# An MLP in Strassen-Winograd form: a tile of its own for the upper weight block, another row of weight steps, two sums on VectorE, and other places for loads where the up phase turns into the down phase

## The chip, the cores and the metric

The kernel runs on one core of a Trainium2 chip. The metric is the device time of one execution in microseconds; of several runs the median counts, and less is better. The names of the engines in the rows are PE (TensorE), PEld (its weight loads), DVE (VectorE), ACT (ScalarE), POOL (GpSimd) and SP (SyncE, which issues nearly all DMAs).

## What is computed

A trunk of two layers on one sequence of 1024 tokens with 1024 channels, all in float32. A layer has a mixing part and then the MLP, which alone is changed here:

```python
h = rms_norm(x, norm2[l])
x = x + jnp.square(jax.nn.relu(h @ w_up[l])) @ w_down[l]
```

`w_up` is 1024 x 4096 and `w_down` 4096 x 1024.

## The kernel before

**Precision.** Every factor of a product is held as two rounded parts, a high part `h` and a low part `l`, and each product is three matmuls: high x high, low x high, high x low (`mm3`). The helper `split` (lines 155 and 156) makes the parts: ScalarE casts the high part, VectorE subtracts it from the source. So every operand costs one ScalarE and one VectorE instruction.

**Strassen-Winograd.** The MLP multiplies 2 x 2 blocks with seven products in place of eight. `STEPS` lists them: for each step the PSUM bank (X, Y or Z), the weight block and the block of the input. The weight blocks A11, A12 and A22 come as they are; S1 to S4 are sums of raw weight blocks. One raw 128 x 1024 tile holds the upper half (`top`: A11, A12), another the lower half (`low`). `weight_steps` returns the named pieces of this work:

- `load`: two DMAs, 512 KB each, into `raw` tiles (two buffers for both halves together);
- `A1`: split of the upper tile (tile names `wh`, `wl`); `s1_s2`: two sums on GpSimd into `s` (lines 828 and 829); `S12`: split of `s` (`wh`, `wl` again);
- `s3_s4`: two differences on GpSimd (lines 835 and 836), the first into `tmp`, the second over the lower tile itself; `S3`: split of `tmp` (`uh`, `ul`); `S4`: split of the lower tile (`vh`, `vl`).

**The up phase** (`for fp in range(NFP)`, 16 periods a layer, 7 steps of 12 matmuls each, so 84 matmuls). While TensorE works on period `fp`, the other engines make the weights of `fp + 1`; `UP_AT` says behind which step of the period each piece is written. A number above 6 means the next period: 7 is its step 0, 8 its step 1. After each product comes its evacuation: ScalarE copies the first use of a bank out (`keep`, line 990: P1 after step 0, U2 after step 2, P5 after step 3), since a later step accumulates on top in the same bank; VectorE adds or subtracts the next one (lines 1040, 1049, 1053) and applies ReLU times the RMS factor (`relu`, line 996), GpSimd squares the result (line 999). `mixed` (line 1011) makes the blocks T1 to T4 from the four squared blocks B11, B12, B21, B22 with four VectorE sums, and the blocks go to DRAM (`hid`); B11 and B21 are stored as two parts (`in_two`). In the last two periods of layer 1 there are no `mixed` blocks.

Within the up phase the order on ScalarE, VectorE and GpSimd is that of the program: `queue` chains each instruction to the one before on its engine. What waits at the head holds all behind it. Elsewhere, and on SyncE and TensorE, a scheduler sets the order when the program is built.

**The down phase** (`for g`, 8 groups in layer 0 and 7 in layer 1, each of two halves `u` of 14 products of 6 matmuls, so 84 matmuls again). VectorE adds each product to the tiles `acc` (line 1105), which hold the residual stream. `load_block` fetches the blocks of the next group (raw in `hr`, then split into the per-block tiles), and `weight_steps` prepares the weights for the next half by `DOWN_AT`.

**The change of phase.** In the last up period the blocks of the first down group are loaded and split, one pair of blocks after each step. Six `acc` tiles are loaded one period before that (`early_acc`), the other ten when the pool `md` of the down phase opens (line 1112).

**The start of the up phase.** The RMS factors need sums of squares over all channels. `rms(1, 0)` (lines 198 to 216) is written behind step 3 of the first period: TensorE sums columns against `ones` (line 198, waiting for GpSimd's last addition), and after a power on GpSimd it spreads the result (line 214). ReLUs written earlier are put off until then (`after_rms`).

## Time and profile before

| | us |
|---|---|
| median of 3 runs | 2311.51 (2309.04 to 2314.63) |
| the profiled execution | 2312.99 |
| span of the profile | 2311.1 |
| TensorE busy | 2160.8 (93%) |
| VectorE busy | 1777.5 (77%) |
| GpSimd busy | 1181.7 (51%) |
| ScalarE busy | 944.8 (41%) |

The page also cuts the span into 40 slices; TensorE's clock is granted in full in most of them. The mean busy share says little about a kernel of many stages. The up phase lies from 466.57 to 827.74 us in layer 0 and from 1600.98 to 1957.67 in layer 1; the down phase follows each. The views used below are busy time by stretch, timelines of single engines, and lists of who waited for whom.

### The profile page before, as it was taken

The page shows a single profiled execution, that of the slowest core. Times are in us where ns is not written, and L with a number is a line of the kernel's source. Part 1 is how long each engine was busy: PE and PEld are TensorE (multiplying, and loading weights), DVE is VectorE, ACT ScalarE, POOL GpSimd, SP SyncE. Part 2 cuts the span into 40 slices and gives each one's busy share as a digit, 9 for nine tenths or more (in the row PEclk, how much of TensorE's full clock was granted, in tenths as well). Part 3 has the DMA queues.
Part 4 walks back from the last instruction along what each step waited for, and adds up shares of the span by engine and source line. Part 5 has one row for each costly group of instructions (what it writes and reads, how often), then busy time and mean ns, then how long its engine had stood idle before and what let it go on. Part 6 is the DMA issues. An engine that isn't in the chain of part 4 may idle for free. (4 is left out here: it accounts for less than half of the span.)

```text
span 2311.1 us, 30279 instructions
## 1 busy us (share of the span) xinstructions
PE 2160.8 (93%) x10608; PEld 1783.2 (77%) x10608; DVE 1777.5 (77%) x2244; ACT 944.8 (41%) x1669; POOL 1181.7 (51%) x915
## 2 busy tenths in 40 slices
PE   7999999979999979999999999998999999899997
PEld 6988887767777767788788888876777777688886
DVE  8788779976666679888868878799666665988864
ACT  5566562532332233333356656435323223433321
POOL 6455556675555633333455646459555555332315
PEclk9999999989999999999999999999999999999998
DMA  3000112234444486554311010133444446765512
GB/s 129 28 28 28 43 33 87 96 128 165 159 171 152 151 298 223 158 193 145 106 50 39 18 46 25 55 87 119 155 154 156 173 157 221 251 194 179 173 55 73
DMA packets 153737, 283.17 MB, mean 123 GB/s; under 512 B 15089, under 2 KB 48369, under 8 KB 153585
## 3 DMA queue, kind: packets, MB, share of 16 engines
q1 hardware_dynamic: 151920, 279.15, 36.1%
q10 hardware_dynamic: 1664, 2.10, 0.3%
q8 instruction: 83, 1.36, 0.2%
q14 instruction: 70, 0.57, 0.1%
HBM read 190.49 MB, written 90.70 MB: 122 GB/s over the span
## 5 line engine op out<-in xcount | busy, mean ns | idle before, releaser
L434 POOL TENSOR_TENSOR a<-a,s 128x255 f32<-128x255 f32 (+1 forms) x192 | 237.2, 1243 | 183.6 <-ACT a L427 100.9
L828 POOL TENSOR_TENSOR s<-raw 128x512 f32<-128x512 f32 x62 | 95.3, 1537 | 457.4 <-DMA raw<-in_w_down 273.9
L999 POOL TENSOR_TENSOR ct<-ct 128x512 f32<-128x512 f32 x128 | 173.7, 1357 | 208.9 <-DVE ct L996 110.2
L156 DVE TENSOR_TENSOR wl<-raw,wh 128x1024 fp32r<-128x1024 f32 x114 | 168.3, 1477 | 48.3 <-ACT wh L155 48.1
L243 PE MATMUL pj<-hB,wh 128*128 128x512 f32 x504 | 198.4, 394 | 0.9 <-ACT hB L880 0.9
L248 PE MATMUL pj<-lB,wh 128*128 128x512 f32 x504 | 197.6, 392 | 1.0 <-DVE lB L881 1.0
L249 PE MATMUL pj<-hB,wl 128*128 128x512 f32 x504 | 197.2, 391 | 0.0
L1011 DVE TENSOR_TENSOR ct<-ct,ct 128x512 f32<-128x512 f32 x120 | 80.4, 690 | 133.2 <-POOL ct L999 132.1
L1105 DVE TENSOR_TENSOR acc<-acc,po 128x512 f32<-128x512 f32 x240 | 159.1, 679 | 19.2 <-PE po L249 18.0
L155 ACT CAST wh<-raw 128x1024 fp32r<-128x1024 f32 x114 | 119.6, 1049 | 100.1 <-PE pj L248 77.9
L155 ACT CAST wh<-s 128x1024 fp32r<-128x1024 f32 x62 | 65.0, 1049 | 206.8 <-POOL s L829 197.6
L155 ACT CAST ct<-ct 128x512 fp32r<-128x512 f32 x64 | 39.7, 620 | 250.4 <-POOL ct L999 250.4
L458 DVE TENSOR_TENSOR tl<-t,th 128x512 fp32r<-128x512 f32 (+1 forms) x160 | 99.0, 629 | 44.4 <-ACT th L456 43.1
L243 PE MATMUL pg<-hB,vh 128*128 128x512 f32 x240 | 98.2, 409 | 37.0 <-ACT ct L990 36.9
L155 ACT CAST hT<-hr 128x512 fp32r<-128x512 f32 x122 | 74.2, 619 | 139.9 <-DMA hr<-hd_T 90.1
L431 DVE TENSOR_TENSOR_SCAN s<-s 128x256 f32<-128x256 f32 (+3 forms) x128 | 123.4, 976 | 6.4 <-ACT s L426 6.1
L156 DVE TENSOR_TENSOR wl<-s,wh 128x1024 fp32r<-128x1024 f32 x62 | 90.6, 1461 | 40.6 <-ACT wh L155 40.6
L835 POOL TENSOR_TENSOR tmp<-raw,raw 128x512 f32<-128x512 f32 x62 | 121.4, 1959 | 0.0
L243 PE MATMUL po<-hT,wh 128*128 128x512 f32 x256 | 105.4, 412 | 9.2 <-ACT ct L990 4.0
L426 ACT ACTIVATE s<-z 128x256 f32<-128x256 f32 (+1 forms) x192 | 95.4, 500 | 45.4 <-PE z L422 13.6
L248 PEld LDWEIGHTS pj<-lB,wh 128*128 128x128 f32 x504 | 94.9, 188 | 21.1 <-DVE lB L881 1.6
L243 PEld LDWEIGHTS pj<-hB,wh 128*128 128x128 f32 x504 | 94.9, 188 | 20.8 <-ACT hB L880 1.3
(274 smaller groups left out, 7094.7 us busy)
## 6 DMA issues: line engine op xcount, KB each, us to landing
raw<-in_w_up SPq DMA_DIRECT2D x64, 512.0 KB, 3.6
raw<-in_w_down SPq DMA_DIRECT2D x64, 512.0 KB, 3.7
hd_T<-ct SPq DMA_DIRECT2D x120, 256.0 KB, 2.8
hr<-hd_T SPq DMA_DIRECT2D x120, 256.0 KB, 3.1
raw<-in_w_in SPq DMA_DIRECT2D x36, 512.0 KB, 3.7
hd_B<-ct SPq DMA_DIRECT2D x34, 256.0 KB, 2.0
hr<-hd_B SPq DMA_DIRECT2D x34, 256.0 KB, 3.5
raw<-in_w_out SPq DMA_DIRECT2D x16, 512.0 KB, 3.6
```

Of the source, the lines that this page charges most:

```text
L155: queue("act", nc.scalar.copy(hi, src))
L156: queue("dve", nc.vector.tensor_sub(lo, src, hi.bitcast(F32)))
L243: mm = nc.tensor.matmul(ps, ah, bh, start=first and i == 0, stop=False, skip_group_check=more)
L248: nc.tensor.matmul(ps, ah, bl, start=False, stop=False, skip_group_check=more)
L249: mm = nc.tensor.matmul(ps, al, bh, start=False, stop=last and i == n - 1, skip_group_check=more)
L426: nc.scalar.activation(s[:, lo:CH], z[:, 0:w], AF.Sigmoid, scale=-ISQ)
L431: nc.vector.tensor_tensor_scan(sl, sl, sl, 1.0 if prev is None else prev[:, CH - 1 : CH], ALU.mult, ALU.bypass)
L434: nc.gpsimd.tensor_mul(a[:, lo + 1 : CH], a[:, lo + 1 : CH], s[:, lo : CH - 1])
L458: nc.vector.tensor_sub(tl[:, 0:wd], pt[:, 0:wd], th[:, 0:wd].bitcast(F32))
L835: queue("pool", nc.gpsimd.tensor_sub(s3, r["a1"][:, 0], r["a2"][:, 0]))
L999: queue("pool", nc.gpsimd.tensor_mul(t, t, t))
L1105: (nc.vector.tensor_add if sign > 0 else nc.vector.tensor_sub)(x, x, ps)
```

## The change

- The upper weight tile gets its own place `rt` (one buffer, pool `mw`); `raw` keeps two buffers for the lower tile alone. To make room, `hr` has 3 buffers in place of 4, and one `acc` tile fewer is loaded early.
- `weight_steps` takes an engine. In the up phase the two differences `s3_s4` go to VectorE; for the first period's weights and in the down phase they stay on GpSimd.
- `UP_AT` has each piece one or two steps earlier.
- The early `acc` loads move from period 14 to period 12; the ten others are eleven now, three at the opening of `md` and the rest written behind steps 1 to 4 of the first half group.
- The raw blocks T2 (both) and T1 (one) of the first down group are loaded from period 14, step 3; B22 and T4 are loaded and split in the first half group in place of the last up period; the blocks of group 1 are all loaded in the second half of group 0 in place of half by half.
- `rms(1, 0)` is written behind step 5 of the first period in place of step 3, and the ReLU of B22 is put off with the others.

```diff
--- before.py
+++ after.py
@@ -797,10 +797,11 @@
                 b = "T1" if b == "B12" else b
                 return t512("h" + b, 4, F32R, pool), t512("l" + b, 4, F32R, pool)
-            def weight_steps(srcs, n, out):
+            def weight_steps(srcs, n, out, eng="pool"):
+                sub = {"pool": nc.gpsimd, "dve": nc.vector}[eng].tensor_sub
                 turns = "p (n k w) -> p k n w"
                 r = {}
@@ -815,11 +816,11 @@
                     return two
                 def load():
-                    raws = []
-                    for src in srcs:
-                        raws.append(per.tile([P, D], F32, tag="raw", name=nm("raw"), bufs=2))
-                        nc.sync.dma_start(raws[-1].rearrange("p (f c) -> p f c", f=src.shape[1]), src)
-                    r["top"], r["low"] = raws
+                    r["top"] = mw.tile([P, D], F32, tag="rt", name=nm("rt"), bufs=1)
+                    r["low"] = per.tile([P, D], F32, tag="raw", name=nm("raw"), bufs=2)
+                    raws = r["top"], r["low"]
+                    for raw, src in zip(raws, srcs):
+                        nc.sync.dma_start(raw.rearrange("p (f c) -> p f c", f=src.shape[1]), src)
                     r["a1"], r["a2"] = (x.rearrange(turns, n=n, k=2) for x in raws)
                 def s1_s2():
@@ -832,8 +833,8 @@
                 def s3_s4():
                     s3 = r["s3"] = tmp()
                     s3 = s3.rearrange("p (n w) -> p n w", n=n)
-                    queue("pool", nc.gpsimd.tensor_sub(s3, r["a1"][:, 0], r["a2"][:, 0]))
-                    queue("pool", nc.gpsimd.tensor_sub(r["a2"][:, 0], r["s2"], r["a1"][:, 1]))
+                    queue(eng, sub(s3, r["a1"][:, 0], r["a2"][:, 0]))
+                    queue(eng, sub(r["a2"][:, 0], r["s2"], r["a1"][:, 1]))
                 return {
                     "load": load,
@@ -847,7 +848,7 @@
-            UP_AT = {"load": 2, "A1": 3, "s1_s2": 3, "s3_s4": 4, "S12": 5, "S3": 7, "S4": 8}
+            UP_AT = {"load": 0, "A1": 2, "s1_s2": 2, "s3_s4": 3, "S12": 4, "S3": 5, "S4": 7}
             DOWN_AT = {"load": 0, "A1": 2, "s1_s2": 2, "S12": 3, "s3_s4": 4, "S3": 4, "S4": 6}
             def up_blocks(fp):
@@ -931,7 +932,7 @@
             acc_, b_next, early_acc = {}, [], []
             for u in range(2):
-                early_acc += [(2 * u + q, c) for c in ((1, 0), (0,))[u] for q in range(2)]
+                early_acc += [(q, 1 - u) for q in range(2)] + [(2, 0)] * u
             def load_acc(m, c, pool):
                 acc_[m, c] = pool.tile([P, CH], F32, name=nm("acc"))
@@ -941,7 +942,7 @@
                 if b in STORED:
                     return None
-                raw = t512("hr", 4, F32, mw)
+                raw = t512("hr", 3, F32, mw)
                 nc.sync.dma_start(raw, hid[fp, b])
                 return raw
@@ -971,7 +972,7 @@
                 for fp in range(NFP):
                     a, a_next = a_next, {}
-                    work = weight_steps(*(up_blocks(fp + 1) if fp < NFP - 1 else down_blocks(0, 0)), a_next)
+                    work = weight_steps(*(up_blocks(fp + 1) if fp < NFP - 1 else down_blocks(0, 0)), a_next, "dve")
                     todo = {k - 7: v for k, v in left.items() if k > 6}
                     for name, f in work.items():
                         todo.setdefault(UP_AT[name], []).append(f)
@@ -979,7 +980,7 @@
                     banks = {"X": pso(), "Y": psj(), "Z": psg() if fp else pso()}
                     kept, hb = {}, {}
                     classic = l == DEPTH - 1 and fp >= NFP - 2
-                    if fp == NFP - 2:
+                    if fp == NFP - 4:
                         for mc in early_acc:
                             load_acc(*mc, mw)
                     if fp == NFP - 1:
@@ -1025,9 +1026,13 @@
                         bank, i = products(a, xb, banks, step, 0)
                         ps = banks[bank]
                         b = STEPS[step][3]
-                        if fp == NFP - 1:
-                            raws = [raw_block(p, b) for p in range(2)]
-                        if step == 3 and fp == 0:
+                        if (fp, step) == (NFP - 2, 3):
+                            raws = {"T2": [raw_block(p, "T2") for p in range(2)], "T1": [raw_block(0, "T1")]}
+                        if (fp, step) == (NFP - 1, 3):
+                            raws["T1"].append(raw_block(1, "T1"))
+                        if (fp, step) == (NFP - 1, 4):
+                            raws["T3"] = [raw_block(p, "T3") for p in range(2)]
+                        if step == 5 and fp == 0:
                             rms(1, 0)
                             rms_done = True
                             for f, args in later:
@@ -1047,7 +1052,7 @@
                             elif (bank, i) == ("X", 2):
                                 t = kept["P5"]
                                 queue("dve", nc.vector.tensor_sub(t, ps, t))
-                                relu("B22", t, t, 0)
+                                after_rms(relu, "B22", t, t, 0)
                             elif (bank, i) == ("Z", 1):
                                 t = kept["U2"]
                                 queue("dve", nc.vector.tensor_sub(t, t, ps))
@@ -1064,9 +1069,9 @@
                                 mixed("T3", "B22", "B12", nc.vector.tensor_sub)
                             elif step == 6:
                                 mixed("T4", "B21", "T2", nc.vector.tensor_sub)
-                        if fp == NFP - 1:
+                        if fp == NFP - 1 and step < 5:
                             for p in range(2):
-                                b_next[p][b] = load_block(p, b, raws[p])
+                                b_next[p][b] = load_block(p, b, raws[b][p] if b in raws else None)
                 for k in sorted(left):
                     if k > 6:
                         for f in left[k]:
@@ -1105,11 +1110,13 @@
                     (nc.vector.tensor_add if sign > 0 else nc.vector.tensor_sub)(x, x, ps)
                 n_groups = groups - (l == DEPTH - 1)
-                for u in range(2):
-                    for i, c in ((0, 1), (0, 0), (2, 0), (2, 1)):
-                        for q in range(2):
-                            if (4 * u + i + q, c) not in acc_:
-                                load_acc(4 * u + i + q, c, md)
+                for mc in ((3, 0), (2, 1), (3, 1)):
+                    load_acc(*mc, md)
+                first_acc = {
+                    k: [(4 + i + q, c) for q in range(2)] for k, i, c in ((1, 0, 1), (2, 0, 0), (3, 2, 0), (4, 2, 1))
+                }
                 for g in range(n_groups):
                     bs, b_next = b_next, [{}, {}]
                     for u in range(2):
@@ -1142,9 +1149,16 @@
                             for name, f in work.items():
                                 if DOWN_AT[name] == step:
                                     f()
-                            if g < n_groups - 1:
-                                b = STEPS[step][3]
-                                b_next[u][b] = load_block(2 * g + 2 + u, b)
+                            b = STEPS[step][3]
+                            if g == u == 0:
+                                for mc in first_acc.get(step, []):
+                                    load_acc(*mc, md)
+                                if step < 2:
+                                    for p in range(2):
+                                        bs[p][STEPS[step + 5][3]] = load_block(p, STEPS[step + 5][3])
+                            elif g < n_groups - 1:
+                                for p in range(2) if g == 0 else (u,):
+                                    b_next[p][b] = load_block(2 * g + 2 + p, b)
                         if g == groups - 1:
                             if u == 1:
                                 order.pop(0)
```

What this makes of the instruction order is shown at three places.

VectorE, one period in the middle of layer 0's up phase, from the sum that makes B11 (`ct_6392`, now `ct_6396`) on; `rbc` is the RMS factor. Before:

```order
L1040 TENSOR_TENSOR ct_6392<-pj_6378,ct_6392 128x512
L996 SCALAR_TENSOR_TENSOR ct_6392<-ct_6392,rbc_5350 128x512
L156 TENSOR_TENSOR vl_6420<-raw_6289,vh_6419 128x1024
L156 TENSOR_TENSOR ct_6438<-ct_6392,ct_6437 128x512
L156 TENSOR_TENSOR wl_6462<-raw_6443,wh_6461 128x1024
L1049 TENSOR_TENSOR ct_6459<-po_6377,ct_6459 128x512
L996 SCALAR_TENSOR_TENSOR ct_6459<-ct_6459,rbc_5357 128x512
L1053 TENSOR_TENSOR ct_6435<-ct_6435,pg_6379 128x512
L996 SCALAR_TENSOR_TENSOR ct_6435<-ct_6435,rbc_5357 128x512
```

Now:

```order
L1045 TENSOR_TENSOR ct_6396<-pj_6382,ct_6396 128x512
L997 SCALAR_TENSOR_TENSOR ct_6396<-ct_6396,rbc_5391 128x512
L156 TENSOR_TENSOR ct_6442<-ct_6396,ct_6441 128x512
L156 TENSOR_TENSOR wl_6448<-rt_6408,wh_6447 128x1024
L836 TENSOR_TENSOR tmp_6468<-rt_6408,raw_6409 128x512
L837 TENSOR_TENSOR raw_6409<-s_1331_6451,rt_6408 128x4x128
L1054 TENSOR_TENSOR ct_6466<-po_6381,ct_6466 128x512
L997 SCALAR_TENSOR_TENSOR ct_6466<-ct_6466,rbc_5398 128x512
L156 TENSOR_TENSOR wl_6488<-s_1331_6451,wh_6487 128x1024
```

The split of the lower tile (`vl`) has left this piece for an earlier one, and the two differences (lines 836 and 837, out of `rt` and `raw`) stand between `wl` and the sum for B22 (line 1054). The second reads `s`, the product of GpSimd's two sums.

TensorE, start of layer 0's up phase; `pj` and `po` are the banks of steps 1, 0 and 2, `rbc_4785` and `rbc_4807` the sums of squares of the two token halves. Before:

```order
L248 MATMUL pj_5270<-lB_1096_5191,wh_5244 128x512
L249 MATMUL pj_5270<-hB_1095_5190,wl_5245 128x512
L198 MATMUL pg_5329<-ones,rbc_4785 128x2 x4
L198 MATMUL pg_5337<-ones,rbc_4807 128x2 x4
L243 MATMUL po_5269<-hT_1003_4863,wh_5251 128x512
```

Now:

```order
L243 MATMUL po_5269<-hB_984_4787,wh_5244 128x512
L248 MATMUL po_5269<-lB_985_4788,wh_5244 128x512
L198 MATMUL pg_5370<-ones,rbc_4785 128x2 x4
L249 MATMUL po_5269<-hB_984_4787,wl_5245 128x512
L243 MATMUL po_5269<-hB_1018_4906,wh_5244 128x512
```

The column sums of the first half, which stood behind the 24 matmuls of steps 0 and 1, stand behind the second matmul of step 0. Those of the other half stay between steps 1 and 2.

SyncE, the change of phase in layer 0; `acc<-xm` are loads of the residual stream, `hr<-hd` raw blocks (138 to 149 belong to group 1). Before:

```order
L1007 DMA hd_B21l<-ct_7874 128x512
L821 DMA raw_7929<-in_w_down 128x4x256
L945 DMA hr_8168<-hd_T_147 128x512
L938 DMA acc_7887<-xm_1_104 128x512
L938 DMA acc_7889<-xm_1_106 128x512
L938 DMA acc_7891<-xm_1_108 128x512
L938 DMA acc_7893<-xm_1_110 128x512
```

Now:

```order
L823 DMA raw_8058<-in_w_down 128x4x256
L1008 DMA hd_B21l<-ct_7852 128x512
L946 DMA hr_8203<-hd_B_139 128x512
L946 DMA hr_8209<-hd_B_149 128x512
L939 DMA acc_7861<-xm_0_107 128x512
L939 DMA acc_7863<-xm_1_104 128x512
L939 DMA acc_7865<-xm_1_106 128x512
L939 DMA acc_7917<-xm_1_108 128x512
L939 DMA acc_7919<-xm_1_110 128x512
```

All eleven later `acc` loads stand in one row here too (four of them are shown), behind loads of group 1's blocks; the first is `acc_7861`, which the first half group adds to.

## Rows read from the trace of the kernel before

**Rows 1.** Busy us by stretch: from:to length, PE PEld DVE ACT POOL, clock, DMA, GB/s.

```profile
466.57:504.84 38.27, 30.28 (x117) 23.66 (x118) 26.96 (x25) 15.65 (x24) 29.45 (x21) 0.78 0.32 112
504.84:803.75 298.91, 278.80 (x1178) 217.58 (x1176) 192.05 (x238) 87.32 (x126) 167.56 (x112) 1.00 0.47 164
803.75:901.06 97.31, 84.88 (x338) 65.39 (x336) 78.30 (x108) 36.04 (x54) 37.08 (x25) 0.95 0.78 265
1057.15:1076.49 19.34, 19.34 (x85) 15.77 (x84) 16.34 (x21) 6.68 (x9) 7.20 (x4) 1.00 0.60 204
1638.70:1936.95 298.25, 278.66 (x1177) 217.54 (x1176) 191.42 (x238) 87.22 (x126) 168.06 (x112) 1.00 0.47 164
1936.95:2028.67 91.72, 81.91 (x337) 63.19 (x336) 75.78 (x98) 35.88 (x54) 35.05 (x25) 0.98 0.77 261
```

**Rows 2.** Timeline of TensorE, one period of the up phase: start us, us, [idle <-releaser].

```profile
1844.13 0.40 PE L249 MATMUL po<-hT,ul 128*128 128x512 f32 x1
...
1845.85 0.50 PE L243 MATMUL pg<-hB,vh 128*128 128x512 f32 x1 [1.32 <-ACT ct L990]
...
1867.20 0.50 PE L243 MATMUL pg<-hB,vh 128*128 128x512 f32 x1 [1.32 <-ACT ct L990]
```

**Rows 3.** Timeline of GpSimd in that period.

```profile
1847.60 1.59 POOL L828 TENSOR_TENSOR s<-raw 128x512 f32<-128x512 f32 x1 [2.93 <-DMA raw<-in_w_up]
...
1852.30 2.27 POOL L835 TENSOR_TENSOR tmp<-raw,raw 128x512 f32<-128x512 f32 x1
1854.65 1.29 POOL L836 TENSOR_TENSOR raw<-s,raw 128x512 f32<-128x512 f32 x1
1855.90 1.04 POOL L999 TENSOR_TENSOR ct<-ct 128x512 f32<-128x512 f32 x1
...
1864.12 1.90 POOL L999 TENSOR_TENSOR ct<-ct 128x512 f32<-128x512 f32 x1 [3.40 <-issue]
```

**Rows 4.** Timeline of VectorE in that period.

```profile
1846.78 1.23 DVE L156 TENSOR_TENSOR wl<-raw,wh 128x1024 fp32r<-128x1024 f32 x1 [0.74 <-ACT wh L155]
...
1852.01 1.41 DVE L156 TENSOR_TENSOR wl<-s,wh 128x1024 fp32r<-128x1024 f32 x1 [0.57 <-ACT wh L155]
...
1856.98 2.02 DVE L1011 TENSOR_TENSOR ct<-ct,ct 128x512 f32<-128x512 f32 x3 [3.56 <-POOL ct L999]
...
1863.29 0.69 DVE L996 SCALAR_TENSOR_TENSOR ct<-ct,rbc 128x512 f32<-128x512 f32 x1
1863.90 1.22 DVE L156 TENSOR_TENSOR vl<-raw,vh 128x1024 fp32r<-128x1024 f32 x1
```

**Rows 5.** Timeline of ScalarE at the end of that period.

```profile
1866.05 0.62 ACT L155 CAST ct<-ct 128x512 fp32r<-128x512 f32 x1 [3.24 <-POOL ct L999]
1866.57 0.58 ACT L990 COPY ct<-pg 128x512 f32<-128x512 f32 x1
1867.05 1.05 ACT L155 CAST wh<-raw 128x1024 fp32r<-128x1024 f32 x1
```

**Rows 6.** Timeline of the DMA issues from SyncE in that period.

```profile
1843.79 0.33 SPq L821 DMA_DIRECT2D raw<-in_w_up  x1
...
1861.88 0.38 SPq L1007 DMA_DIRECT2D hd_B21h<-ct  x1
...
1865.14 0.33 SPq L821 DMA_DIRECT2D raw<-in_w_up  x1
```

**Rows 7.** The loads of line 821 by source line, whole run.

```profile
DMA to landing us min/median/max: 3.3/3.6/7.6
```

**Rows 8.** Timeline of TensorE in the first up period of layer 0.

```profile
478.49 1.86 PE L198 MATMUL pg<-ones,rbc 128*128 128x2 f32 x8 [2.61 <-POOL rbc L187]
...
485.71 0.80 PE L243 MATMUL po<-hT,wh 128*128 128x512 f32 x1 [2.01 <-ACT ct L990]
```

**Rows 9.** Timeline of TensorE in the first down half group of layer 0.

```profile
838.96 0.78 PE L249 MATMUL po<-hT,wl 128*128 128x512 f32 x1 [3.36 <-DVE wl L156]
```

**Rows 10.** Waits of GpSimd from 1936 to 2029: us in total, times, longest.

```profile
POOL s L828 <- DMA raw<-in_w_down: 33.9, 3, 12.1
```


## The prediction

> **What bounds the kernel now.** The first view is the busy time by stretch [rows 1]. In the down phase 84 matmuls take 19.34 us with TensorE busy all of it: that is the floor of a period. Up periods are the same 84 matmuls, but 14 of them take 298.91 us in layer 0 and 298.25 in layer 1. At the floor they would take 270.8, so 28.1 and 27.5 us are lost there. The change of phase (last up period and three half groups, four times the floor, 77.4 us) takes 97.31 and 91.72, so 19.9 and 14.3 are lost. The first up period takes 38.27 us at a granted clock of 0.78.
>
> The second view, TensorE's timeline [rows 2], shows where an up period loses: the fourth bank use waits 1.32 us for ScalarE's copy of P5, and this repeats after 21.35 us (1867.20 less 1845.85). The reader is to see that the pitch is the same to 0.01 us: something turns in a ring of 21.35 us.
>
> The third view finds the ring. On ScalarE the copy of P5 (1866.57) stands behind the cast of B11, which waited 3.24 us for GpSimd's square [rows 5]. On GpSimd [rows 3] the period begins with 2.93 us of waiting for the lower weight tile; then follow the two sums, the square of B22, the two differences and, at 1855.90, the square of B12. VectorE waits 3.56 us for that one before it makes T1 to T3 [rows 4]; B21, T4, B11 follow, and the split `vl` at 1863.90 ends at 1865.12. It frees the lower tile: the next load is issued at 1865.14, and the one before was at 1843.79 [rows 6], again 21.35 apart. From issue to GpSimd's first sum are 3.81 us (1847.60 less 1843.79). So **the ring is load, GpSimd, VectorE, load**, and TensorE hangs on it.
>
> The rows also show that GpSimd and VectorE take turns. The difference at 1852.30 takes 2.27 us where the next takes 1.29; `wl` at 1852.01 takes 1.41 where the one at 1846.78 takes 1.23 [rows 3, 4]. Together the two last from 1852.01 to 1854.57, 2.56 us, about the 1.23 + 1.29 that they take one by one.
>
> **Part 1: the up phase.** With `rt` and two buffers for the lower half, a load no longer waits for `vl`: the old ring is cut. GpSimd loses two instructions a period (1.29 us each alone), VectorE gains two. No row shows these differences on VectorE; the nearest are T1 to T3, 128 x 512 out of SBUF, three in 2.02 us, so I take 0.65 each. What is late next is VectorE's own queue, which is in program order. I lay it out from the start of B11's ReLU (time 0), with 1.14 for a wide split, 0.60 for a narrow one, 1.25 for a GpSimd sum and turns where both want to run:
>
> - ReLU 0.69 [rows 4]; square on GpSimd 0.13 later, 1.04 [rows 3]: 1.86. Cast 0.62, then `wh` half a microsecond after the cast began, 1.05 [rows 5]: 3.5.
> - Meanwhile the lower tile lands. Its issue stands behind the store of B21's high part, in the old rows 1.13 us after that cast began (1861.88 less 1860.75); issued 0.44 later, landed after 3.81, it is there at about 2.3. So: first sum to 3.6, B11's low part to 4.1, second sum to 5.4, `wl` to 6.5, the two differences to 7.85.
> - Sum and ReLU of B22 1.35; `wl` of S1 and S2 1.14; sum and ReLU of B12 1.4, with 0.3 for the square of B22 in between; `ul` 0.6: 12.65. Square of B12 1.04: 13.7.
> - T1 to T3 1.97; ReLU of B21 0.68; square 1.13; T4 0.64; `vl` 1.14; B21's low part 0.6; sum for B11 0.72: 20.5.
>
> The same way of counting gives 9.6 us from the first sum to the end of B12's square in the old period, where the rows have 9.34 (1847.60 to 1856.94): 2 to 3% too much. So I take **20.1 us a period** for 21.35. It lies above the floor, so the new ring still decides, and TensorE's wait shrinks from 2.0 to 0.75 us. The first of the 14 periods starts with a lead and stays near 19.85; then 19.85 + 13 x 20.1 = 281.2, against 298.91 and 298.25: **-35 us** for both layers. Bounds: at the floor -57; at 20.8 (one more turn lost to a GpSimd instruction of 0.7) -17.
>
> On the turns, the Trainium skill ("SBUF — State Buffer", section "SBUF: two separate sides") says that GpSimd and a VectorE instruction with two SBUF inputs share a port pair as an exclusive lock, held for a whole instruction. It speaks against this change, since two more such instructions come onto VectorE beside GpSimd's two sums. Taken strictly it would leave the 20.5 uncorrected, and this part would be -25; the trace agrees but for those 2 to 3%.
>
> The other moves of this part: `UP_AT` puts splits earlier, and ScalarE, busy 87.32 of 298.91 us [rows 1], has room for them; the load of `rt` waits for the second difference (7.85), lands near 12.5 and is wanted only a period later; the stores behind it on SyncE wait for blocks that come later anyway. These count as nothing.
>
> **Part 2: the change of phase.** Now the first half group waits up to 3.36 us for `wl` [rows 9], since GpSimd waited for `raw<-in_w_down`, 12.1 us the longest [rows 10]. Loads of line 821 normally land after 3.6 us, here after up to 7.6 [rows 7]. With the load at step 0 and two more steps of lead this wait goes. What is late next is VectorE: 78.30 of 97.31 us busy [rows 1]. In layer 0 the scheduler pulls group 1's splits into the first half group. I count there 14 additions, 11 low parts, 5 short leftovers and `ul` (31 at about 0.63) and three wide ones (1.2): 23.1, with turns 24.5, above the floor. In layer 1 it is 21 short and two wide, 15.6: I take 21 for that half group. The last up period I put at 22 and 20, since it has six low parts and casts ahead of the copy of P5, the other two halves at 19.5. Layer 0: 22 + 24.5 + 39 = 85.5, layer 1: 20 + 21 + 39 = 80: **-23 us**. Bounds: all of the loss gone -34, little gained -8.
>
> **Part 3: the first up period.** The column sums now stand behind the second matmul, and TensorE stops there until GpSimd's last addition, before at 478.43 (the matmul waited to 478.49, [rows 8]). Then 22 matmuls follow, at 0.23 us each (19.34 / 84) with the clock in full and twice that at half, 5.1 to 10.1 us: step 2 would start between 483.6 and 488.6, not at 485.71 [rows 8], -2.1 to +2.9. On the other hand that addition has one GpSimd instruction fewer ahead of it, and the copy of P5 no longer stands behind squares. I take 0 for each layer, bounds -3 and +3.
>
> **Sum.** -35 - 23 + 0 = -58 on the profiled execution, 2312.99, which is 1.5 above the median of 2311.51. On the median: **2254 us**. A measurement can tell from no change what differs by over 0.2%, 4.6 us.
>
> **Rivals.**
> - *TensorE bounds the up phase.* If VectorE's and GpSimd's turns overlap more than I counted, for instance since the first sum fits into the 1.6 us in which VectorE waits for the cast, the ring falls to 19.4 or less and everything up to the floor is won: -54 there, and with the change of phase about 2233. For it: with durations taken alone the queue above sums to 18 us. Against it: the 2.27 and 1.41 of [rows 3, 4].
> - *The spreading does not happen.* In the queue of SyncE the late `acc` loads still stand in one row, now behind loads of group 1 that wait for VectorE's splits, and with them VectorE's additions to (3, 0). Then Part 2 gives nothing and Part 3 its +3: about 2279. For it: the order as built. Against it: they are issued 0.4 us apart, and the largest waits there were for weights, not for `acc`.
> - *VectorE is stuck behind a late load: slower.* Its second difference now waits for GpSimd's second sum, and so for the lower tile, with the evacuations of B22 and B12 and T1 to T4 queued behind it. Each microsecond that the tile lands later than 2.3 lengthens the ring by as much. From 5.1 us of landing time (3.81 + 1.25) the up phase gains nothing, from about 5.9 what Part 2 wins is lost too; at 6.5 the ring is 22.8, 26 periods lose 1.45 each, and the kernel takes 2311.5 + 38 - 23, some 2326. For it: 7.6 was seen [rows 7]. Against it: 3.6 is the median, and DMA engines are busy 0.47 in these stretches [rows 1].
>
> **Chances.** The forecast (ring of about 20.1) 0.60; TensorE bounds 0.18; no spreading 0.15; late load 0.07. Three of the four are faster: 0.92; within 0.2% 0.02; slower 0.06. The range goes from 2228 (the first rival with a change of phase better by 5) to 2292 (ring of 20.8, -17; change of phase -8; start +6), which leaves out the last rival and the ends of the others.
>
> **What would show it.** Right: no wait of GpSimd for `raw<-in_w_up` in the up phase; up periods of 20.1 with a TensorE wait of some 0.5 us for the copy of P5; no wait for `wl` in the first half group. Periods of 19.4 mean the first rival; periods over 21 with VectorE idle before line 837 mean the third. Wrong altogether: periods as before, or waits for `acc` in the down phase.

## The result, and the profile after

The changed kernel takes 2273.75 us (median of 4 runs, 2272.71 to 2277.84), the kernel before 2313.07 beside it (4 runs). The ratio is 0.9831, with a 95% interval of 0.9816 to 0.9847: 39 us less. The profiled execution of the changed kernel took 2273.57 us, with a span of 2271.7.

The forecast was 2254, so the gain came out at two thirds of what it said. Where it went is seen by stretch (start of one period to the start of another, TensorE's first matmul; both layers apart):

| stretch | before | after | difference | forecast |
|---|---|---|---|---|
| 14 up periods, layer 0 | 298.91 | 276.44 | -22.5 | -17.7 |
| 14 up periods, layer 1 | 298.25 | 276.41 | -21.8 | -17.1 |
| change of phase, layer 0 | 97.31 | 104.37 | **+7.1** | -11.8 |
| change of phase, layer 1 | 91.72 | 94.17 | **+2.5** | -11.7 |
| all the rest | | | -4.6 | 0 |

The up phase gained more than was forecast; the change of phase lost where it should have gained. The same view as [rows 1], for the kernel after (from:to length, PE PEld DVE ACT POOL, clock, DMA, GB/s):

```profile
503.25:779.69 276.44, 274.80 (x1177) 219.61 (x1176) 217.03 (x268) 90.64 (x126) 118.07 (x85) 1.00 0.53 177
779.69:884.06 104.37, 85.27 (x337) 67.20 (x336) 85.64 (x110) 35.50 (x52) 35.54 (x24) 0.89 0.73 244
1619.45:1895.86 276.41, 274.93 (x1178) 219.61 (x1176) 217.00 (x268) 90.60 (x126) 118.00 (x85) 1.00 0.53 177
1895.86:1990.03 94.17, 82.53 (x337) 65.58 (x336) 79.34 (x100) 35.01 (x52) 35.42 (x24) 0.93 0.75 254
```

VectorE is now busy 217.03 us of the 14 up periods where it was 192.05 [rows 1], and GpSimd 118.07 where it was 167.56: the two differences have moved. In the change of phase the granted clock has fallen from 0.95 and 0.98 to 0.89 and 0.93.

**The up phase.** The first of the 14 periods takes 20.82 us, the other 13 take 19.67 each (nearly all of them 21.35 before). One of them on VectorE's timeline, from the sum that makes B11 on (line 1045; as in [rows 4]):

```profile
650.12 0.68 DVE L1045 TENSOR_TENSOR ct<-pj,ct 128x512 f32<-128x512 f32 x1
650.84 0.69 DVE L997 SCALAR_TENSOR_TENSOR ct<-ct,rbc 128x512 f32<-128x512 f32 x1
653.39 1.14 DVE L156 TENSOR_TENSOR ct<-ct,ct 128x512 fp32r<-128x512 f32 x1 [1.86 <-ACT ct L155]
654.45 2.32 DVE L156 TENSOR_TENSOR wl<-rt,wh 128x1024 fp32r<-128x1024 f32 x1
656.69 0.68 DVE L836 TENSOR_TENSOR tmp<-rt,raw 128x512 f32<-128x512 f32 x1
657.47 0.69 DVE L837 TENSOR_TENSOR raw<-s,rt 128x512 f32<-128x512 f32 x1
658.08 0.68 DVE L1054 TENSOR_TENSOR ct<-po,ct 128x512 f32<-128x512 f32 x1
...
663.61 0.69 DVE L1012 TENSOR_TENSOR ct<-ct,ct 128x512 f32<-128x512 f32 x1 [0.94 <-POOL ct L1000]
```

GpSimd's timeline in the same period (as in [rows 3]):

```profile
651.66 1.04 POOL L1000 TENSOR_TENSOR ct<-ct 128x512 f32<-128x512 f32 x1 [3.92 <-ACT ct L991]
652.66 1.32 POOL L829 TENSOR_TENSOR s<-raw 128x512 f32<-128x512 f32 x1
654.05 1.63 POOL L830 TENSOR_TENSOR s<-s,rt 128x512 f32<-128x512 f32 x1
```

GpSimd's first sum no longer waits for a load: 2.93 us of waiting stood before it in [rows 3], now it follows B11's square at once. The issues of the lower tile's load from SyncE show why:

```profile
629.96 0.33 SPq L823 DMA_DIRECT2D raw<-in_w_up  x1
...
649.63 0.33 SPq L823 DMA_DIRECT2D raw<-in_w_up  x1
```

The load at 649.63 still goes out right behind a `vl`, which ends at 649.60. But it takes 4.3 us to land, to about 653.9, and the sum has begun at 652.66: the sum reads the tile that was loaded a period earlier, at 629.96. With both `raw` buffers for lower tiles, the load of one has nearly a whole period to spare.

The list of waits of VectorE in the 13 periods (us in total, times, longest) has two lines only:

```profile
DVE ct L1012 <- POOL ct L1000: 27.9, 26, 1.2
DVE ct L156 <- ACT ct L155: 24.2, 13, 1.9
```

So VectorE never waits for TensorE there, and TensorE (busy 274.80 of 276.44) waits a little for VectorE once a period:

```profile
PEld po L243 <- DVE ct L1054: 6.2, 13, 0.5
```

**The change of phase.** All waits of TensorE of over 0.6 us in the change of phase of layer 0 (first four rows) and of layer 1:

```profile
804.87 0.79 PE L243 MATMUL po<-hT,vh 128*128 128x512 f32 x1 [8.25 <-DVE ct L1054]
818.30 0.47 PE L243 MATMUL po<-hT,wh 128*128 128x512 f32 x1 [3.01 <-DVE acc L1110]
821.22 0.80 PE L243 MATMUL po<-hT,wh 128*128 128x512 f32 x1 [0.87 <-DVE acc L1110]
839.29 0.80 PE L243 MATMUL pg<-hB,vh 128*128 128x512 f32 x1 [6.90 <-DVE acc L1110]
1918.72 0.80 PE L243 MATMUL po<-hT,vh 128*128 128x512 f32 x1 [6.12 <-DVE ct L1054]
1933.53 0.77 PE L243 MATMUL po<-hT,wh 128*128 128x512 f32 x1 [4.88 <-DVE acc L1110]
```

The wait for `wl` of [rows 9] is gone; waits for VectorE stand in its place. The first, 8.25 us before the last step of the last up period, is for the sum of B22 (line 1054). What holds VectorE there stands in the timelines of VectorE, of ScalarE and of SyncE's issues:

```profile
803.52 0.69 DVE L156 TENSOR_TENSOR lT<-hr,hT 128x512 fp32r<-128x512 f32 x1 [5.89 <-ACT hT L155]
804.13 0.68 DVE L1054 TENSOR_TENSOR ct<-po,ct 128x512 f32<-128x512 f32 x1
```

```profile
802.88 0.62 ACT L155 CAST hT<-hr 128x512 fp32r<-128x512 f32 x1 [8.86 <-DMA hr<-hd_T]
```

```profile
795.61 0.48 SPq L1008 DMA_DIRECT2D hd_B11h<-ct  x1
796.29 0.32 SPq L1008 DMA_DIRECT2D hd_B11l<-ct  x1
796.92 1.77 SPq L946 DMA_DIRECT2D hr<-hd_T  x2
...
831.50 6.81 SPq L939 DMA_DIRECT2D acc<-xm  x11
```

The second raw block of T1 finds the three `hr` buffers taken by T2, T2 and T1. It is issued at 796.92, behind two stores, and ScalarE casts it at 802.88. VectorE's low part of it (803.52) stands in program order ahead of the sum of B22, for which TensorE waits. The last of these rows is the other thing to see: all eleven late `acc` loads go out in one row, the first at 831.50. TensorE stops at 832.4 for an addition that needs it, the one to (3, 0); VectorE makes it at 838.56, behind two low parts of group 1's blocks:

```profile
835.39 3.25 DVE L156 TENSOR_TENSOR lB<-hr,hB 128x512 fp32r<-128x512 f32 x2 [0.75 <-ACT hB L155]
838.56 0.67 DVE L1110 TENSOR_TENSOR acc<-acc,pg 128x512 f32<-128x512 f32 x1
```

### The profile page after: what moved, and what is told of

Read it like the earlier page. It is cut to its first block, busy times and chain, and to the rows that moved or that the text cites. A ratio compares the mean times of both kernels' runs of the same rounds, so it can differ in the third digit from the quotient of the medians.

```text
span 2271.7 us, 30343 instructions
## 1 busy us (share of the span) xinstructions
PE 2144.4 (94%) x10608; PEld 1787.6 (79%) x10608; DVE 1830.7 (81%) x2308; ACT 952.0 (42%) x1669; POOL 1070.8 (47%) x851
## 5 line engine op out<-in xcount | busy, mean ns | idle before, releaser
L836 POOL TENSOR_TENSOR tmp<-rt,raw 128x512 f32<-128x512 f32 x30 | 48.6, 1618 | 344.0 <-DMA rt<-in_w_down 332.1
L249 PE MATMUL pj<-hB,wl 128*128 128x512 f32 x504 | 197.7, 392 | 0.0
L248 PE MATMUL pj<-lB,wh 128*128 128x512 f32 x504 | 197.7, 392 | 0.0
L991 ACT COPY ct<-po 128x512 f32<-128x512 f32 x66 | 38.8, 588 | 267.0 <-PE po L249 260.5
L243 PE MATMUL po<-hB,wh 128*128 128x512 f32 x248 | 99.3, 400 | 26.0 <-ACT wh L155 26.0
L243 PE MATMUL po<-hT,vh 128*128 128x512 f32 x248 | 103.0, 415 | 17.5 <-DVE ct L1054 16.2
L156 DVE TENSOR_TENSOR wl<-rt,wh 128x1024 fp32r<-128x1024 f32 x62 | 110.6, 1784 | 7.1 <-ACT wh L155 7.0
L249 PEld LDWEIGHTS pj<-hB,wl 128*128 128x128 f32 x504 | 94.9, 188 | 19.9
L156 DVE TENSOR_TENSOR lT<-hr,hT 128x512 fp32r<-128x512 f32 x122 | 97.7, 806 | 14.7 <-ACT hT L155 14.6
L156 DVE TENSOR_TENSOR ct<-ct,ct 128x512 fp32r<-128x512 f32 x64 | 57.2, 893 | 60.0 <-ACT ct L155 60.0
```

The lines of the kernel that those rows point to most:

```text
L156: queue("dve", nc.vector.tensor_sub(lo, src, hi.bitcast(F32)))
L243: mm = nc.tensor.matmul(ps, ah, bh, start=first and i == 0, stop=False, skip_group_check=more)
L248: nc.tensor.matmul(ps, ah, bl, start=False, stop=False, skip_group_check=more)
L249: mm = nc.tensor.matmul(ps, al, bh, start=False, stop=last and i == n - 1, skip_group_check=more)
```

## The experiments

Twelve kernels ran. Ratios are to the kernel before on the same chip. The last three columns are from the traces: an up period (the median of the 13; before 21.35, after 19.67), the change of phase of both layers together (before 189.0, after 198.5), and where the 14 up periods of layer 0 begin. Each kernel has one trace. Where a kernel has lines added, its line numbers are up to 10 higher.

| run | median, us | ratio (95%) | up period | change of phase | begins |
|---|---|---|---|---|---|
| e1_loads_as_before | 2274.39 | 0.9836 (0.9817 to 0.9855) | 19.67 | 197.5 | 503.3 |
| e2_diff_on_gpsimd | 2276.48 | 0.9843 (0.9823 to 0.9863) | 19.73 | 200.7 | 504.0 |
| e3_t1_in_tmp | 2268.77 | 0.9811 (0.9790 to 0.9831) | 19.67 | 193.7 | 507.0 |
| e4_t1_and_hold | 2267.82 | 0.9804 (0.9789 to 0.9820) | 19.67 | 187.7 | 507.4 |
| e5_six_early | 2272.69 | 0.9830 (0.9812 to 0.9849) | 19.66 | 188.8 | 508.9 |
| e6_t1_six_hold | 2260.47 | 0.9780 (0.9763 to 0.9797) | 19.66 | 172.8 | 507.7 |
| e7_tile_alone | 2297.76 | 0.9946 (0.9925 to 0.9967) | 20.54 | 197.7 | 505.5 |
| e8_old_steps | 2276.86 | 0.9852 (0.9835 to 0.9870) | 19.90 | 195.0 | 504.6 |
| e9_first_top_in_raw | 2278.59 | 0.9853 (0.9839 to 0.9868) | 19.67 | 196.3 | 506.6 |
| e10_all_mended | 2250.51 | 0.9732 (0.9716 to 0.9748) | 19.67 | 175.8 | 502.3 |
| e11_before_hr3 | 2317.96 | 1.0022 (1.0010 to 1.0034) | 21.34 | 193.0 | 504.9 |
| e12_diff_one_later | 2271.31 | 0.9803 (0.9789 to 0.9817) | 20.30 | 177.6 | 506.8 |

### What shortened the up period: tile, steps or the two differences

The own tile alone, on the kernel before:

```diff
-raws.append(per.tile([P, D], F32, tag="raw", name=nm("raw"), bufs=2))   # both halves
+r["top"] = mw.tile([P, D], F32, tag="rt", name=nm("rt"), bufs=1)
+r["low"] = per.tile([P, D], F32, tag="raw", name=nm("raw"), bufs=2)
-raw = t512("hr", 4, F32, mw)
+raw = t512("hr", 3, F32, mw)
```

> The kernel before with the own place for the upper tile alone (hr at 3 buffers): old UP_AT, differences on GpSimd, old loads, old place of the column sums. Theory A (the ring was the lower tile's load waiting for vl, and the own tile alone cuts it): up periods of 19.7 to 20.1 and the whole gain of the change, about 2274 (2268 to 2282). Theory B (the tile only helps together with the earlier weight steps, since with the old ones the load of a lower tile is written behind step 2, and GpSimd starts as late as before): periods of 20.7 to 21.3, 2295 to 2313.

The periods lie between the two ranges, 20.54 us, and the time in B's: the tile alone brings 0.81 of the 1.68 us, and the change of phase gets 8.6 us longer (197.7 for 189.0). That is nearly all of the 9.5 us that the changed kernel loses there, with none of its other edits.

The changed kernel with the differences on GpSimd (`a_next, "pool"`), and with the old `UP_AT`:

> The changed kernel with the two differences s3_s4 back on GpSimd in the up phase; own weight tile, new UP_AT and new loads stay. Theory A (the ring was cut by the own tile, and the engine of the differences matters little): up periods stay at 19.4 to 19.9, the kernel within 4 us of 2273.6, or some us faster, since VectorE has 1.3 us less to do in the last up period. Theory B (GpSimd would bound the ring with them: sums, differences and squares with their waits): up periods of 20.3 to 20.8, so 13 x 2 x 0.8 = 21 us more, about 2294.

> The changed kernel with the old UP_AT; own tile, differences on VectorE and new loads stay. Theory A (the own tile is what counts): up periods of at most 19.9, within 5 us of 2273.7. Theory B (the earlier steps count): periods of 20.4 or more, 2290 or more. In the last up period fewer weight steps lie before the splits of T1 and T3, so the change of phase may differ by some us either way.

Theory A both times, nearly to the full: 19.73 and 19.90. With the own tile, either the earlier steps (e2) or the differences on VectorE (e8) bring most of the rest, and both together little more than the steps alone. Neither was tried without the tile. Moving the two differences has nearly no effect, because they cost VectorE's queue about as much on either engine. The groups of GpSimd's instructions in the 13 up periods of e2 (busy us, mean ns of one | idle before):

```profile
L836 POOL TENSOR_TENSOR tmp<-rt,raw 128x512 f32<-128x512 f32 x13 | 29.6, 2278 | 0.0
L837 POOL TENSOR_TENSOR raw<-s,rt 128x512 f32<-128x512 f32 x13 | 21.1, 1627 | 1.0
```

That is 3.9 us on GpSimd for 1.37 on VectorE (656.69 and 657.47 above). But while they run on GpSimd, VectorE's split out of `s` is stretched:

```profile
659.54 2.32 DVE L156 TENSOR_TENSOR wl<-s,wh 128x1024 fp32r<-128x1024 f32 x1
```

where it takes 1.22 in the changed kernel. So VectorE is busy 218.10 us of layer 0's 14 periods in e2, with two instructions fewer a period, and 217.03 in the changed kernel. The Trainium skill ("Perfetto Trace Analysis", section "Optimizing Scalar/DVE Operations") says that offloading between these two engines might not help, since they share a port of SBUF. This pair of runs agrees: 19.67 and 19.73.

**Is 19.67 TensorE's floor plus a bit of waiting, or a ring?** The last run took the mended kernel (below) and wrote the differences one step later, behind the sum of B22:

```diff
-UP_AT = {"load": 0, "A1": 2, "s1_s2": 2, "s3_s4": 3, "S12": 4, "S3": 5, "S4": 7}
+UP_AT = {"load": 0, "A1": 2, "s1_s2": 2, "s3_s4": 4, "S12": 4, "S3": 5, "S4": 7}
```

> The mended run with the two differences written behind step 4 in place of step 3, so behind the sum and ReLU of B22 in VectorE's queue. Theory A (what is left over the floor in an up period, 19.67 against 19.35, is TensorE waiting 0.3 us for the sum of B22, which stands behind the two differences; no ring is left, VectorE idles 4 us a period): periods of 19.35 to 19.4, 26 x 0.3 = 8 us less, about 2242 us. Theory B (a ring through VectorE of 19.67 still sets the period; the later differences free the lower tile later): periods of 19.6 to 20.1, 2248 to 2262.

Theory A falls, and with it my own reading that 4 us of idle time on VectorE were slack. The period is 20.30 and the kernel 21 us slower than the mended one. TensorE no longer waits for B22 but for the copy of P5, as in [rows 2]:

```profile
623.33 0.53 PE L250 MATMUL pg<-hB,vh 128*128 128x512 f32 x1 [0.69 <-ACT ct L1001]
```

VectorE's waits are the same as after, at most 1.2 us for GpSimd's squares and 1.9 for the cast of B11. They are answers to its own instructions and lie inside its ring. What has grown is its work: in its new place the first difference runs beside GpSimd's square of B22 and takes 1.53 us, where it took 0.68:

```profile
626.64 1.95 POOL L1010 TENSOR_TENSOR ct<-ct 128x512 f32<-128x512 f32 x1 [2.49 <-DVE ct L1007]
```

```profile
627.62 1.53 DVE L846 TENSOR_TENSOR tmp<-rt,raw 128x512 f32<-128x512 f32 x1
```

VectorE is busy 226.28 us of layer 0's 14 periods where it was 217.09 in the mended kernel, 0.66 more a period, and the period is 0.63 longer. VectorE's queue with these answers is what sets the up period.

### Why the change of phase did not get shorter

The changed kernel, with all loads and splits of the change of phase where they were before:

> The changed kernel, but with every load and split of the change of phase where the kernel before has them (hr stays at 3 buffers, five early acc). Theory A (the new places of the loads made the change of phase longer: 104.37 and 94.17 us in place of 97.31 and 91.72): the up phase keeps its 276.4 us, the change of phase goes back to about 97 and 92, and the kernel to about 2264 us (2258 to 2268). Theory B (the two differences on VectorE and the weight steps made it longer, whatever the loads): no change, 2270 to 2278. If even the forecast's 85 and 80 were hidden by the new places: about 2240.

Theory B for the whole: 2274.39, and 197.5 us where the changed kernel has 198.5. So the new places explain neither the 23 us that were to be won nor the 9.5 that were lost. Nor do the other runs bear out theory B's cause: with the differences back on GpSimd (e2) the change of phase takes 200.7 us, and with neither the differences nor the new steps (e7) 197.7. And the stall of the last up period is there with the old places too, 7.80 us at 804.67; ScalarE waits for the same kind of load:

```profile
ACT hT L155 <- DMA hr<-hd_T: 9.1, 2, 8.4
```

With three `hr` buffers the old places have the stall as well. That buffer alone, in the kernel before:

```diff
-raw = t512("hr", 4, F32, mw)
+raw = t512("hr", 3, F32, mw)
```

> The kernel before with hr at 3 buffers in place of 4 and nothing else. Theory A (the buffer given up is what made the last up period longer: the fourth raw block waits for a place and VectorE for it): the last up period goes from 23.99 and 20.72 us to about 30 and 27, and the kernel to some 2320 to 2328. Theory B (the shorter up periods leave VectorE with a backlog there, and the buffer costs little): 2309 to 2315.

The stall appears as theory A says, in TensorE's row, and the last up period goes from 23.99 to 33.88 us and from 20.72 to 32.49:

```profile
832.38 0.80 PE L243 MATMUL po<-hT,vh 128*128 128x512 f32 x1 [9.76 <-DVE ct L1049]
```

But the kernel loses only 4.5 us, between the two theories' ranges, and the change of phase 4.0. The first half group shrinks from 31.23 to 22.30 and from 27.77 to 21.22: TensorE waits 1.11 us there for an addition and 0.40 for `ul`, and the wait for `wl` of [rows 9] is gone. The one wait has taken the place of the other.

Now the other way, each late thing of the changed kernel taken away. T1's second raw block in a free `tmp` tile, loaded with the first:

```diff
-raws = {"T2": [...], "T1": [raw_block(0, "T1")]}
+raws = {"T2": [...], "T1": [raw_block(0, "T1"), raw_block(1, "T1", True)]}   # True: out of tmp()
-if (fp, step) == (NFP - 1, 3):
-    raws["T1"].append(raw_block(1, "T1"))
```

> The changed kernel, but the second raw block of T1 for the first down group has a free tmp tile and is loaded together with the first, one period earlier. Theory A (VectorE stands still in the last up period because this block's load waits for a buffer and then behind two stores; the evacuation of B22 is queued behind its split): the stall of TensorE of 8.3 us in layer 0 and 6.1 in layer 1 goes, and with VectorE ahead the first half group of layer 0 loses its stalls of 3.4 and 1.5 too: about 2255 us (2250 to 2261). Theory B (VectorE has too much to do in these periods in any case, and what waits here is only waited for later): 2268 to 2274.

Half of it: the last up period falls from 29.98 to 22.07 and from 27.17 to 20.17, but the first half group grows from 35.67 to 37.87 and from 26.91 to 33.98. The kernel gains 5 us, not 18. What the first half group waits for is now one long stall, 8.79 us at 836.72, for the addition to (3, 0).

The splits of group 1's blocks held behind the last addition of the first half group, on top of that:

```diff
+if behind[1] is not None:   # in split(), for group 1's blocks alone
+    tc.add_manual_dep(op.ins, behind[1], ...)   # behind[1]: last addition of the first half group
```

> As the run with T1's block in a tmp tile, and besides the low parts of group 1's blocks may not go ahead of the last addition of the first half group in VectorE's queue. Theory A (the stall of 7.3 us in layer 0 and 5.3 in layer 1 late in the first half group is VectorE working on group 1's blocks while additions wait behind): some 10 us less than the run before, about 2245 us. Theory B (the work only moves: the second half group then waits for VectorE as long): the same as the run before within 4 us.

Theory B by the median (1 us), although in the traces the change of phase is 6.0 us shorter; the traced execution of e3 is the slowest of its four. What keeps it from being 10 us less stands in the trace. VectorE's timeline and the issues from SyncE, layer 0:

```profile
827.88 0.67 DVE L1115 TENSOR_TENSOR acc<-acc,pg 128x512 f32<-128x512 f32 x1
833.20 0.69 DVE L1115 TENSOR_TENSOR acc<-acc,pg 128x512 f32<-128x512 f32 x1 [4.65 <-DMA acc<-xm]
```

```profile
827.38 0.32 SPq L1015 DMA_DIRECT2D hd_B21l<-ct  x1
827.80 6.97 SPq L946 DMA_DIRECT2D acc<-xm  x11
```

With everything else out of the way VectorE is idle, and waits for the tile (3, 0) itself. Its load is issued behind the last store of a `ct` tile (827.38): the eleven tiles lie in `md`, which opens on the memory of the up phase's `ct` tiles. Before the change (3, 0) was among the six early tiles; as the sixth, it was given up for `rt`. It fits, though. The changed kernel with six early tiles:

```diff
-early_acc += [(q, 1 - u) for q in range(2)] + [(2, 0)] * u
+early_acc += [(2 * u + q, c) for c in ((1, 0), (0,))[u] for q in range(2)]
```

> The changed kernel, but acc (3,0) is loaded early again, as the sixth tile in mw; nothing else is changed. Theory A (the stall of 7.3 us in layer 0 and 5.3 in layer 1 in the first half group is the load of this tile: its place is one of the up phase's ct tiles, so it is issued behind the last store of period 15, at 831.5 in layer 0): these stalls shrink by half or more, about 2266 us (2262 to 2270). Theory B (VectorE's splits of group 1 ahead of the addition take as long, they ended at 838.6): no gain, 2271 to 2276.

In the change of phase theory A: 188.8 for 198.5, and the first half group of layer 0 takes 26.70 in place of 35.67. In the kernel's time theory B: 2272.69. Of the 9.8 us, 5.6 are given back ahead of layer 0's 14 periods, which begin at 508.9 in place of 503.25 (below); the profiled execution has a span of 2266.8 for 2271.7, and the median shows less than that. All three together:

> The run with T1's block in tmp and the hold on group 1's splits, and besides acc (3,0) loaded early. Theory A (there VectorE waited 4.65 us in layer 0 and 0.96 in layer 1 for that load with nothing else to do): some 7 us less than the 2267.8 of that run, about 2261. Theory B (the additions of (2,1) and (3,1), whose loads stand in the same row, then wait as long two steps later): 2265 to 2268.

2260.47, theory A, with a change of phase of 172.8 us. Against the changed kernel that is 25.8 less, while the T1 block alone brought 4.8, the six tiles alone 9.8, and the hold 6.0 on top of the T1 block. Three waits stand one behind another in VectorE's queue, and each one taken away uncovers the next.

### The first up period

`rt` lies in a pool whose memory the mixing part gives back late: in the changed kernel its first load is issued at 467.93, behind seven stores of that part, where the lower tile's goes at 446.60. TensorE's rows there, from the last matmul of the mixing part:

```profile
460.10 0.39 PE L249 MATMUL po<-yh,wl 128*128 128x512 f32 x1
473.26 0.80 PE L243 MATMUL po<-hB,wh 128*128 128x512 f32 x1 [12.77 <-ACT wh L155]
...
478.75 0.79 PE L249 MATMUL po<-hB,wl 128*128 128x512 f32 x1 [2.57 <-DVE wl L156]
```

So the first upper tile went back into `raw`:

```diff
-for step in weight_steps(*up_blocks(0), a_next).values():
+for step in weight_steps(*up_blocks(0), a_next, own=False).values():   # top in raw
```

> The changed kernel, but the upper weight tile of the very first up period lies in a raw tile, as before, and not in rt. Theory A (rt lies in memory that the mixing part gives back late, so its first load is issued at 467.9 in layer 0 where the raw tile's was at 448.4, and TensorE waits 13.2 us for its cast): step 0 of the first period starts near 467 in place of 473.3, and each layer gains 3 to 5 us: about 2266. Theory B (GpSimd's last addition to the sums of squares, at 478, decides when the period goes on, whatever was done before it): 0 to 2 us in all, 2271 to 2275.

By the time theory B, and not even that: 2278.59, some 5 us more. Step 0 does start earlier, at 469.41, but then the column sums stand behind 24 matmuls again, and TensorE waits for GpSimd's last additions there, as at 478.49 in [rows 8]:

```profile
465.14 0.40 PE L249 MATMUL po<-yh,wl 128*128 128x512 f32 x1
...
481.30 1.87 PE L198 MATMUL pg<-ones,rbc 128*128 128x2 f32 x8 [2.61 <-POOL rbc L187]
484.64 1.87 PE L198 MATMUL pg<-ones,rbc 128*128 128x2 f32 x8 [1.48 <-POOL rbc L187]
488.52 0.80 PE L243 MATMUL po<-hT,wh 128*128 128x512 f32 x1 [2.00 <-ACT ct L994]
```

In e5, e6 and e7 the scheduler put all column sums ahead of step 0, though only e7 touches a line of this stretch. In e5 TensorE waits 13.80 and 4.19 us there without a product done:

```profile
477.01 3.58 PE L198 MATMUL pg<-ones,rbc 128*128 128x2 f32 x16 [13.80 <-POOL rbc L187]
484.78 1.44 PE L214 MATMUL pg<-ident,rst 128*128 128x128 f32 x5 [4.19 <-POOL rst L204]
```

The traces separate this stretch from what comes before it. Its length, in us, from the end of the last matmul of the mixing part (460.49 in the changed kernel, 465.54 in e9) to the start of the 14 periods:

| column sums, first upper tile | kernels | layer 0 | layer 1 |
|---|---|---|---|
| behind 24 matmuls, in `raw` | before, e11 | 42.1 to 42.2 | 41.6 to 41.8 |
| behind the second matmul, in `rt` | after, e1 to e4, e8 | 41.3 to 42.8 | 41.3 to 42.8 |
| ahead of step 0, in `rt` | e5, e6, e7 | 43.7 to 45.7 | 44.2 to 44.3 |
| behind 24 matmuls, in `raw`, with the change's other edits | e9, e10, e12 | 40.4 to 41.1 | 40.3 to 41.0 |

So e9 lost nothing in this stretch: it is 1.7 us shorter in each layer than in the changed kernel (41.08 for 42.76, 41.02 for 42.72) and a little shorter than in any kernel with `rt`. With e5's order it is 2.9 and 1.6 longer. What made e9 slower lies ahead of it: its mixing part in layer 0 ends 5.05 us later, though no line of that part was changed. The same is seen in e3, which has the changed kernel's order of instructions on all engines up to here: its mixing part ends at 465.68, 5.2 us later. What moves the mixing part stays open.

### All of it together

The three mends, both raw blocks of T3 in `tmp` too, and the first upper tile in `raw`:

> The run with T1's block in tmp, the hold and six early acc, and besides both raw blocks of T3 in tmp (loaded at step 0 of the last up period) and the first upper tile in raw. Theory A (each of the late loads found so far cost what the traces show: in the run before this, 3.7 us for T3 in layer 1 and some 3 to 5 us a layer in the first up period): about 2248 us (2242 to 2254). Theory B (VectorE's count of work alone bounds what is left of these stretches): 2257 to 2262.

2250.51 us, theory A by the time: a ratio of 0.9732 (0.9716 to 0.9748) to the kernel before, and 23 us less than the change as it was made. This is the best version of the study. Of the 10 us over e6, 7.1 lie in the two stretches of the table above (40.40 for 43.68 and 40.44 for 44.22), where both the tile's place and the place of the column sums differ; T3's blocks gained nothing (175.8 against 172.8). What is left, by stretch:

```profile
502.30:778.79 276.49, 274.83 (x1178) 219.62 (x1177) 217.09 (x268) 90.60 (x126) 118.07 (x85) 1.00 0.54 180
778.79:869.63 90.84, 79.38 (x337) 62.40 (x336) 84.25 (x106) 35.07 (x52) 35.03 (x24) 1.00 0.77 263
1877.72:1962.69 84.97, 79.27 (x337) 62.46 (x336) 78.81 (x99) 35.08 (x52) 36.11 (x24) 1.00 0.79 266
```

In layer 0 VectorE is busy 84.25 of 90.84 us, more than TensorE's floor of 77.4: by this count its work would be the next bound there, which no run tests.

## Why the prediction was right and wrong, step by step

The sign and the range held, the range in part by luck: Part 2 came out 33 us worse than forecast, outside its own bounds (-34 to -8), and 9 us more from Part 1 and 4.6 from all the rest made up for some of it.

- **The ring (load, GpSimd, VectorE, load) and that it is cut: right.** GpSimd does not wait for `raw<-in_w_up` in any of the 13 periods. The words "a load no longer waits for `vl`" are not right: it is still issued 0.03 us behind it (649.63), but for the sum of the next period.
- **"A new ring above the floor, through VectorE's own queue": right in kind**, by e12 and the list of VectorE's waits. **20.1 us a period was mis-sized: 19.67.** The layout had 20.5 before it was taken down. Counted from B11's ReLU (650.84), it had the differences done at 7.85 and the square of B12 at 13.7; the rows have 7.32 (658.16) and 12.77 (663.61). From there on 6.8 and 6.9 agree. Of the 0.9 too much, 0.5 is the lower tile, which I let land at 2.3 for this sum: it is there a period before, and GpSimd's first sum starts at 1.82 without a wait. Another 0.3 is the square of B22, which holds up only 0.1 (0.81 us for the ReLU at 661.26). The part gave -44.3 us, not -35.
- **The rule weighed there.** B11's low part starts at 653.39 and takes 1.14, where a 128x512 sum without GpSimd beside it takes 0.69 (663.61): GpSimd's first sum lasts to 653.98. `wl` starts at 654.45 and ends at 656.77, 1.09 behind the end of the second sum at 655.68, and 1.2 is what such a split takes by itself. So the Trainium skill ("SBUF — State Buffer", section "SBUF: two separate sides") agrees with the rows: whoever comes second waits for the whole instruction of the other. The -25 that I worked out with it came out too small because of the tile's landing and the square of B22, not because of the rule.
- **The first rival (TensorE bounds) came nearer with its period (19.4) than the forecast, but its mechanism doesn't hold**: TensorE waits for VectorE in each period. Its example holds in part: 0.73 of the 1.32 us of GpSimd's first sum lie in VectorE's wait for the cast (652.66 to 653.39).
- **Part 2: the step that failed.** "With the load at step 0 and two more steps of lead this wait goes. What is late next is VectorE": the wait for `wl` did go. But I summed VectorE's instructions as if all their inputs were there, and put 22 and 20 on the last up period; it took 29.98 and 27.17. The diff takes a buffer from `hr` and makes (3, 0) a late tile, and the sum priced neither; only the second rival named (3, 0). They are behind the 8.25 and 6.12 us for T1's block and, with group 1's low parts, behind the 6.90 and 4.88 in the first half group. With the late loads mended the change of phase is 172.8 to 175.8, against 165.5 in the forecast and 198.5 in the changed kernel: the count itself was 7 to 10 us too low. That lies in the half groups; the last up periods of the mended kernel take 22.08 and 20.18, as counted.
- **The second rival (the spreading does not happen) came true**: eleven `acc` loads in one row, and VectorE's addition to (3, 0) waiting for the first of them (4.65 us in e4, where nothing else hides it). Its price for the part was nothing; by e1 the new places indeed gain nothing, and the +9.5 stands with the old places too (197.5). `rt` and the `hr` buffer given up for it are enough for it, since e7 with these alone has 197.7; in the changed kernel (3, 0) is behind part of it as well (e5). That VectorE's added work counts in it is not shown: e2 has that work on GpSimd and 200.7.
- **Part 3: right by its number, but not by its working.** The 14 periods of layer 0 begin 1.6 us earlier, but the mixing part ends 2.2 us earlier there; from its last matmul on, the stretch is 0.6 and 1.1 us longer than before. Step 0 starts 6.7 us later (473.26 for 466.57), since `rt` is loaded late, and the waits for the column sums that follow in [rows 8] are gone.
- **The third rival (a late lower tile) didn't come.**

## What to carry to other kernels

When an edit makes room for a tile, price what it takes the room from: look up which load used that buffer and what stands behind its consumer in the engine's queue. Where several late loads stand in one in-order queue, taking one away shows little, so find them all in the trace before judging any. And idle time of an engine is slack only if what it waits for does not hang on that engine itself.

## What was unexpected of the hardware

TensorE's granted clock followed the long stalls. In the change of phase of layer 0 it was 0.89 in the changed kernel, where TensorE stood still for 8.25 and 6.90 us; the matmul behind such a stall takes 0.79 or 0.80 us where the others of its kind take 0.40 to 0.50, so it runs at the lower of the two levels, 1.2 for 2.4 GHz. In the mended kernel, with no stall over 2.6 us in these stretches, the clock was 1.00 in both layers, and the same 337 matmuls kept TensorE busy 79.38 us in place of 85.27. So the stalls cost some 6 us more than they last.

With the same order of instructions on all engines up to there, the mixing part of layer 0 ended 5.2 us apart in the traces of two kernels (460.49 in the changed kernel and 465.68 in e3). That is more than the 0.2% that I took for the resolution of the whole measurement, and what moves it was not found. With one trace of each kernel, what an edit brings in a stretch has to be measured from the end of the one before it.
